# Down projections of two feed-forward blocks by seven quarter products instead of eight, with the sums of weight quarters made by adding DMAs

## The chip, the cores and the metric

The kernel runs on one core of a Trainium2 chip. Its time is device microseconds of one execution; a median of several executions is compared. TensorE (PE in the profile, PEld its weight load) does the matrix products, VectorE (DVE) and ScalarE (ACT) the element-wise work, GpSimd (POOL) some small operations, SyncE (SP) issues most DMAs. Each engine runs its own instructions in a fixed order and waits for the others by semaphores.

## The reference

Two layers over 512 tokens of width 1024, all in float32. Layer 0 mixes tokens by retention and neighbourhood attention, layer 1 by a state-space scan (SSD); the changed code is in the feed-forward block that follows each mixer.

```python
def conv_geglu_ffn(hn, w_up, conv_w, conv_b, w_down):
    u = depthwise_conv_centered(hn @ w_up, conv_w, conv_b)
    gate, val = jnp.split(u, 2, axis=-1)
    return (jax.nn.gelu(gate, approximate=True) * val) @ w_down

def reference(x, ...):
    for layer in range(DEPTH):              # 2
        hn = rms_norm(x, norm_mix_pre[layer])
        m = retention_na_mixer(hn, ...) if layer % 2 == 0 else ssd_mixer(hn, ...)
        x = x + rms_norm(m, norm_mix_post[layer])
        f = conv_geglu_ffn(rms_norm(x, norm_ffn_pre[layer]), ffn_w_up[layer], ffn_conv_w[layer],
                           ffn_conv_b[layer], ffn_w_down[layer])
        x = x + rms_norm(f, norm_ffn_post[layer])
    return x
```

The down projection is H (512 tokens x 2816) times w_down (2816 x 1024).

## The kernel before

The program is written in the order mixer 0, `ffn` of layer 0, mixer 1, `ffn` of layer 1; a tile scheduler derives each engine's order from it and from priorities, and sets the semaphores. Tokens lie in four tiles of 128 (t = 0 to 3), the inner dimension in k-tiles of 128.

Every large matrix product is made of three: each operand is split into a high part (rounded to the matmul's reduced float32, by a ScalarE copy) and a low part (what is left, by a VectorE subtract; `split`, L95 and L96), and `mm3` (L104 to L106) sums high x high, low x high and high x low in one PSUM bank.

Weights come as tiles of 128 x 1024 float32 (512 KiB) through `wload`: SP issues the load into one of three staging buffers (`wst`), `wunit` splits it into one of four pairs `whi`/`wlo`, with `high_priority(60)`, so that these splits stand early in the orders of ScalarE and VectorE.

In `ffn` the up projection goes over 22 steps f; a step computes gate and value columns (128 each) for all 512 tokens, 2 x 8 x 3 = 48 matmuls of 512 columns. `tail` does the convolution, the GELU and the product, and splits the result at once into `hh` and `hl`, the k-tile f of H.

`down_tm` then computes the down projection by halves n of 512 output columns: for each batch of weight tiles, four token tiles, 22 k-tiles x 3 matmuls in a bank per token tile and half. That is 528 matmuls of 128 x 512 for each layer. The last batch has six weight tiles, whose last parts are put in buffers of H that are free (`extra`). After a half of a token tile, `post_half` takes the sum of squares (ScalarE, Square, `junk`) and the product with the gain (VectorE, `mg`). `finish` has the steps x (`post_norm`: residual), s (the pre-norm of what follows, or the store of the output) and t (`turn`: eight TensorE transposes into `pt`, split into the residents `xh`/`xl`, from which the next mixer or projection reads). A norm goes through POOL twice: `r_m` and `r_x` are the inverse roots. Their places:

```python
DOWN = ("x0 s0", "x1 s1 t0", "x2 s2 t1", "x3 s3")
LATE = ("t2", "t3")
```

t0 is turned after token tile 1's part of the last batch, t2 and t3 are left to the following stage (`E.late`, `flush`).

Where they stand beside the change: in mixer 0 `project` makes a projection and its rotary part, in which POOL multiplies a rotated copy `rb` (L444) after SP's DMAs `rb<-ra`; in mixer 1 `project` makes the projections of a group, and POOL adds squares (`sq`). POOL issues no DMA.

## Time and profile before

| what | value |
|---|---|
| time of three executions | 1411.16 us median, 1410.93 to 1412.15 |
| span of the profiled execution | 1409.7 us |
| granted TensorE clock | 0.999 |
| PE, PEld, DVE, ACT, POOL busy | 1386.0, 1144.1, 905.1, 710.4, 62.7 us |
| DMA | 166.36 MB, mean 118 GB/s |
| matmuls of the down projections | 2 x 528 |

The span runs from the first to the last instruction of one profiled execution; the time around it is in the timed runs too. Busy matmul time is modelled and overlaps, so it is a sign of TensorE being fed and no peak rate. In a group's row the columns are line, engine, operation, names out<-in, shapes and count, then busy us and mean ns of one, then the idle time of the engine before them and who ended it. In a timeline row the first two numbers are start and length in us, and the bracket is the idle time before it with what ended it.

### The profile page before, as it was taken

How to read it: one execution, taken by the hardware profiler on the slowest of the kernel's cores; microseconds unless marked ns; L12 is line 12 of the kernel's file. 1: busy time of each engine (PE TensorE's matmuls, PEld its weight loads, DVE VectorE, ACT ScalarE, POOL GpSimd, SP SyncE). 2: the span in 40 equal slices, each digit the busy share in tenths (PEclk: the TensorE clock that was granted, in tenths of full speed). 3: DMA queues.
4: the chain of work that ended last, by engine and by line, in shares of the span. 5: the costliest groups of instructions: out<-in, count | busy, mean ns of one | idle time of the engine just before them, and what ended most of it. 6: DMA issues, size and time to landing. Idle time of an engine off the chain costs nothing.

```text
span 1409.7 us, 18020 instructions
## 1 busy us (share of the span) xinstructions
PE 1386.0 (98%) x6908; PEld 1144.1 (81%) x6908; DVE 905.1 (64%) x1364; ACT 710.4 (50%) x1203; POOL 62.7 (4%) x66
## 2 busy tenths in 40 slices
PE   7999999999999999999999999999999999999998
PEld 6877787898888888888778787787888888888886
DVE  7378888755566652347878786897786565654232
ACT  5356665544444431324877787477454444442230
POOL 0010110100000000000000110010110000000000
PEclk9999999999999999999999999999999999999999
DMA  8443233222333233333566454273433333232231
GB/s 291 147 141 96 87 97 101 86 86 92 103 91 104 90 90 109 115 113 106 142 185 189 136 182 146 75 212 107 137 120 105 105 90 105 91 105 90 90 105 60
DMA packets 56438, 166.36 MB, mean 118 GB/s; under 512 B 6688, under 2 KB 7456, under 8 KB 56352
## 3 DMA queue, kind: packets, MB, share of 16 engines
q1 hardware_dynamic: 48464, 150.00, 34.0%
q10 hardware_dynamic: 7888, 15.21, 3.8%
q8 instruction: 55, 0.90, 0.3%
q14 instruction: 31, 0.25, 0.1%
HBM read 157.57 MB, written 5.51 MB: 116 GB/s over the span
## 4 chain that ended last, share of the span: by engine, by line
PE 88%; DVE 4%; ACT 3%; DMA 2%; issue 1%; POOL 1%; SPq 0%; DVEq 0%; POOLq 0%; ACTq 0%
PE mm L104 26%; PE mm L106 26%; PE mm L105 26%; PE pi L844 1%; PE st L793 1%; PE py L864 1%; PE pt L161 1%; PE pt L737 1%; PE y L519 1%; ACT pb L823 1%; DMA pb<-pd 0%; ACT junk L141 0%; DMA x<-in_x 0%; DVE wlo L96 0%; ACT whi L95 0%
## 5 line engine op out<-in xcount | busy, mean ns | idle before, releaser
L104 PE MATMUL mm<-xh,whi 128*128 128x512 f32 (+1 forms) x1216 | 463.9, 382 | 0.4 <-ACT xh L95 0.2
L105 PE MATMUL mm<-xh,wlo 128*128 128x512 f32 (+2 forms) x1216 | 462.8, 381 | 1.4 <-DVE wlo L96 1.4
L106 PE MATMUL mm<-xl,whi 128*128 128x512 f32 (+2 forms) x1216 | 463.2, 381 | 0.5 <-DVE xl L96 0.5
L96 DVE TENSOR_TENSOR wlo<-wst,whi 128x1024 fp32r<-128x1024 f32 (+1 forms) x208 | 254.3, 1224 | 137.3 <-ACT whi L95 135.6
L95 ACT CAST whi<-wst 128x1024 fp32r<-128x1024 f32 (+1 forms) x208 | 216.6, 1042 | 147.1 <-PE mm L105 117.7
L104 PEld LDWEIGHTS mm<-xh,whi 128*128 128x128 f32 x1216 | 228.3, 188 | 45.2 <-issue 2.5
L105 PEld LDWEIGHTS mm<-xh,wlo 128*128 128x128 f32 (+1 forms) x1216 | 228.4, 188 | 44.7 <-DVE wlo L96 1.9
L106 PEld LDWEIGHTS mm<-xl,whi 128*128 128x128 f32 (+1 forms) x1216 | 228.1, 188 | 45.0 <-issue 1.3
L251 DVE SCALAR_TENSOR_TENSOR cv<-mm,cwt,cv 128x511 f32<-128x511 f32 x88 | 65.9, 749 | 146.2 <-ACT cv L250 146.2
L250 ACT ACTIVATE cv<-mm,cwt 128x512 f32<-128x512 f32 x88 | 68.7, 780 | 124.5 <-PE mm L106 124.5
L104 PE MATMUL mm<-whi,hh 128*128 128x512 f32 x288 | 112.0, 389 | 0.0
L105 PE MATMUL mm<-whi,hl 128*128 128x512 f32 x288 | 112.0, 389 | 0.0
L106 PE MATMUL mm<-wlo,hh 128*128 128x512 f32 x288 | 112.0, 389 | 0.0
L823 ACT ACTIVATE pb<-pb,tok 128x128 f32<-128x128 f32 x256 | 80.7, 392 | 6.9 <-DMA pb<-pd 5.5
L95 ACT CAST hh<-cv 128x512 fp32r<-128x512 f32 x44 | 27.3, 621 | 103.7 <-DVE cv L259 103.7
L252 DVE SCALAR_TENSOR_TENSOR cv<-mm,cwt,cv 128x511 f32<-128x511 f32 x88 | 66.0, 750 | 3.0
L105 PEld LDWEIGHTS mm<-whi,hl 128*128 128x128 f32 x288 | 54.1, 188 | 11.3
L104 PEld LDWEIGHTS mm<-whi,hh 128*128 128x128 f32 x288 | 54.1, 188 | 11.2
L106 PEld LDWEIGHTS mm<-wlo,hh 128*128 128x128 f32 x288 | 54.1, 188 | 11.2
L757 DVE SCALAR_TENSOR_TENSOR xf<-mm,cwt,xf 128x511 f32<-128x511 f32 (+1 forms) x64 | 47.5, 744 | 6.4 <-ACT xf L754 5.9
L96 DVE TENSOR_TENSOR hl<-cv,hh 128x512 fp32r<-128x512 f32 x44 | 30.5, 693 | 28.9 <-ACT hh L95 28.9
L141 ACT ACTIVATE junk<-mm 128x512 bf16<-128x512 f32 x24 | 14.3, 596 | 67.4 <-PE mm L106 67.3
(267 smaller groups left out, 1871.7 us busy)
## 6 DMA issues: line engine op xcount, KB each, us to landing
wst<-in_f_up SPq DMA_DIRECT2D x88, 512.0 KB
wst<-in_f_down SPq DMA_DIRECT2D x44, 512.0 KB
wst<-in_c_fm SPq DMA_DIRECT2D x40, 512.0 KB
pb<-pd ACTq DMA_DIRECT2D x29, 512.0 KB
wst<-in_ab_fm SPq DMA_DIRECT2D x20, 512.0 KB
gain<-yd SPq DMA_DIRECT2D x32, 256.0 KB
wst<-in_c_out SPq DMA_DIRECT2D x16, 512.0 KB
gain<-in_norms SPq DMA_DIRECT2D x8, 512.0 KB
```

Of the source, the lines that this page charges most:

```text
L95: first = self.nc.scalar.copy(hi, src)
L96: second = self.nc.vector.tensor_tensor(lo, src, hi.bitcast(F32), op=ALU.subtract)
L104: mm(out, lh, rh, start=first, stop=False)
L105: mm(out, ll, rh, start=False, stop=False)
L106: mm(out, lh, rl, start=False, stop=last)
L141: self.nc.scalar.activation(self.junk[:, :w], src, AF.Square, scale=float(n) ** -0.5, accum_out=s)
L161: last = nc.tensor.transpose(pt[:, j], xs[:, j * P:(j + 1) * P], self.ident)
L250: nc.scalar.activation(o, ps, AF.Identity, scale=w(1), bias=w(3))
L251: nc.vector.scalar_tensor_tensor(o[:, 1:], ps[:, :S - 1], w(0), o[:, 1:], op0=ALU.mult, op1=ALU.add)
L252: nc.vector.scalar_tensor_tensor(o[:, :S - 1], ps[:, 1:], w(2), o[:, :S - 1], op0=ALU.mult, op1=ALU.add)
L757: nc.vector.scalar_tensor_tensor(r[:, a], ps[:, b], wc(j), r[:, a], op0=ALU.mult, op1=ALU.add)
L823: nc.scalar.activation(pb[:, dr, c], pb[:, dr, c], AF.Identity, scale=1.0 - 2 * dr, bias=tok[:, 0, c, dr * H + h:dr * H + h + 1])
```

## The change

H stays float32 as `H`, unsplit. `down_strassen` cuts H into four quarters (lower and upper 256 tokens, first and second 11 k-tiles) and w_down into four quarters (11 k-tiles x 512 columns). Seven products of quarters (or of sums of quarters) replace the eight; each has 11 k-tiles x 2 token tiles x 3 = 66 matmuls, 462 for each layer. Products are numbered 0 to 6 in the order of `seq`.

- Weight sides: products 0, 3 and 6 read quarters of w_down, products 1, 2, 4 and 5 read sums from a DRAM tile `ts`. `sums` lists 32 DMAs ("chores") per layer of 704 KiB each: 16 plain copies from w_down into `ts`, and 16 that add to `ts` in DRAM. POOL issues them, and `E.chore` makes each wait for the last matmul of the projection emitted before (`E.product`). 15 of layer 0's stand in mixer 0 and 17 in the up projection of layer 0, followed there by 12 of layer 1's; the other 20 of layer 1's stand in mixer 1.
- H sides: `prepare` makes the operand of the next product after the second weight tile of a product: `raw` combines quarters on VectorE (products 1, 2 and 6; operations of 2816 columns), and two splits (1280 and 1536 columns) make it high and low. Odd products use `xh`/`xl`'s memory, even ones a pair b1h/b1l. The first operand is split during the up projection, at f = 14.
- Each product loads five weight tiles of 1024 columns and one of 512; every fourth staging tile is an extra one, `wx`.
- Results: the six banks of products 0 to 2 are copied to `k00` to `k21` (ScalarE), and later products' banks are added to them (VectorE, L380); product 6's banks hold the rest. `post_half` takes a sign.
- Turns: t0's transposes stand after the first token tile of product 6 (before its second token tile's first weight tile), t1's before its fourth weight tile. Six weight tiles of product 6 are all asked for ahead of it, two of them into free memory (`x1`, `x2`).
- At the end of mixer 1, t3's transposes stand 8 to 11 matmuls of 256 columns earlier in the next up projection.

```diff
+    def operands(self):
+        self.xh, self.xl = (self.res.tile([P, KD, S], R32, name=n, tag=n) for n in ("xh", "xl"))
+    def chore(self, n=1):
+        for _ in range(min(n, len(self.chores))):
+            self.together([self.chores.pop(0)()], [self.product])
...
-    def mm3(self, out, lh, ll, rh, rl, first, last):
-        mm = self.nc.tensor.matmul
+    def mm3(self, out, lh, ll, rh, rl, first, last, more=False):
+        mm = partial(self.nc.tensor.matmul, skip_group_check=True) if more else self.nc.tensor.matmul
         mm(out, lh, rh, start=first, stop=False)
         mm(out, ll, rh, start=False, stop=False)
-        mm(out, lh, rl, start=False, stop=last)
+        self.product = mm(out, lh, rl, start=False, stop=last)
...
-        (eng or nc.vector).tensor_tensor(m, ps, g_post[:, n * 512:(n + 1) * 512], op=ALU.mult)
-        halves.append((s, m, r))
+        halves = st.setdefault(t, {})
+        for other, _ in halves.values():
+            halves["r"] = self.inv_rms("m", other, s), None
+            break
+        gs = g_post[:, n * 512:(n + 1) * 512]
+        if sign == 1.0:
+            (eng or nc.vector).tensor_tensor(m, ps, gs, op=ALU.mult)
+        else:
+            nc.vector.scalar_tensor_tensor(m, ps, sign, gs, op0=ALU.mult, op1=ALU.mult)
+        halves[n] = s, m
...
+def quarters(w, i):
+
+    return [w[i, 2 * P * S * u:2 * P * S * (u + 1)].rearrange("(p c) -> p c", p=P) for u in range(HK // 2)] + \
+        [w[i, 2 * P * S * (HK // 2):QUARTER].rearrange("(p c) -> p c", p=P)]
+
+def sums(E, w, ts):
+
+    gp = E.nc.gpsimd
+    rows, n = QUARTER // 1024, 4
+    part = lambda a, i, c: a[i].rearrange("(r e) -> r e", e=1024)[c * rows // n:(c + 1) * rows // n]
+    out = []
+    for stage in (((0, w, 0, None), (1, w, 1, None), (2, w, 3, None), (3, w, 2, None)),
+                  ((0, w, 1, ALU.add), (1, w, 3, ALU.add)), ((2, ts, 0, ALU.add),), ((3, ts, 2, ALU.add),)):
+        for i, src, j, op in stage:
+            for c in range(n):
+                kw = dict(accum_op=op, max_dma_last_dim=4096) if op else {}
+                out.append(lambda i=i, src=src, j=j, c=c, kw=kw: gp.dma_start(part(ts, i, c), part(src, j, c), **kw))
+    return out
+
+def down_strassen(E, pool, w, ts, H, first, g_post, done):
+
+    nc, tc = E.nc, E.tc
+    lower, upper = slice(0, HW), slice(HW, S)
+    A11, A21 = H[:, :HK, upper], H[:, :HK, lower]
+    A12, A22 = H[:, HK:, upper], H[:, HK:, lower]
+    k0 = [0]
+
+    def stage(i, u, cols):
+        st = pool.tile([P, 1024], F32, name="wx") if k0[0] % 4 == 3 else E.wst.tile([P, 1024], F32, name="wst")
+        k0[0] += 1
+        nc.sync.dma_start(st[:, :cols], quarters(*i)[u])
+        return st[:, :cols]
+
+    def weights(i, u, extra=None):
+        cols = 1024 if u < HK // 2 else 512
+        st = stage(i, u, cols)
+        if extra is None:
+            hi, lo = E.whi.tile([P, 1024], R32, name="whi"), E.wlo.tile([P, 1024], R32, name="wlo")
+        else:
+            hi, lo = extra[:, :1024], extra[:, 1024:]
+        with tc.high_priority(60):
+            E.split(hi[:, :cols], lo[:, :cols], st)
+        return [(hi[:, c:c + 512], lo[:, c:c + 512]) for c in range(0, cols, 512)]
+
+    a, bb = ([E.mm.tile([P, 512], F32, name="mm") for _ in range(2)] for _ in range(2))
+    s3 = pool.tile([P, HK, HW], F32, name="s3")
+    d = []
+
+    def raw(i):
+        tt, stt = nc.vector.tensor_tensor, nc.vector.scalar_tensor_tensor
+        if i == 1:
+            tt(s3, A11, A21, op=ALU.subtract)
+            return s3
+        if i == 2:
+            tt(A21, A22, A21, op=ALU.subtract)
+            stt(A11, A11, -1.0, A21, op0=ALU.mult, op1=ALU.subtract)
+            return A11
+        if i == 6:
+            stt(A11, A12, -1.0, A11, op0=ALU.mult, op1=ALU.subtract)
+            return A11
+        return {3: A12, 4: A21, 5: A22}[i]
+
+    def prepare(i):
+        if i % 2:
+            hi, lo = (E.res.tile([P, HK, HW], R32, name="a" + n, tag=n) for n in ("xh", "xl"))
+        else:
+            hi, lo = (pool.tile([P, HK, HW], R32, name="a" + n, tag=n) for n in ("b1h", "b1l"))
+        src = raw(i)
+        for c in (slice(0, 5), slice(5, HK)):
+            E.split(hi[:, c], lo[:, c], src[:, c])
+        return hi, lo
+
+    seq = ((w, 0), a), ((ts, 1), bb), ((ts, 2), a), ((w, 2), d), ((ts, 0), a), ((ts, 3), bb), ((w, 3), a)
+    kept = {}
+    st = {}
+    op, nxt = first, None
+    started = []
+    for i, (src, bank) in enumerate(seq):
+        last = i == len(seq) - 1
+        if not bank:
+            bank.extend(E.px.tile([P, 512], F32, name="pd", tag="px") for _ in range(2))
+        more = any(bank is x for x in started)
+        started.append(bank)
+
+        def mms(t, ws, u):
+            for j, w_ in enumerate(ws):
+                k = 2 * u + j
+                cc = slice(t * P, t * P + P)
+                E.mm3(bank[t], op[0][:, k, cc], op[1][:, k, cc], *w_, not more and k == 0, k == HK - 1, more)
+
+        if last:
+            ex = {4: pool.tile([P, 2048], R32, name="x1", tag="s3"), 5: pool.tile([P, 2048], R32, name="x2", tag="e2")}
+            ws = [weights(src, u, ex.get(u)) for u in range(HK // 2 + 1)]
+            for t in range(2):
+                for u, x in enumerate(ws):
+                    if (t, u) == (1, 0):
+                        E.operands()
+                        E.finish("t0", st, done)
+                    if (t, u) == (1, 3):
+                        E.finish("t1", st, done)
+                    mms(t, x, u)
+                E.post_half(st, 2 + t, 1, bank[t], g_post, sign=-1.0)
+                E.finish(f"x{2 + t} s{2 + t}", st, done)
+            continue
+        for uu in ((0,), (1,), (2,), (3,), (4, 5)):
+            ws = [(weights(src, u), u) for u in uu]
+            for t in range(2):
+                for x, u in ws:
+                    mms(t, x, u)
+            if uu == (1,):
+                nxt = prepare(i + 1)
+        op = nxt
+        for t in range(2):
+            if i in (0, 1, 2):
+                kept[i, t] = pool.tile([P, 512], F32, name=f"k{i}{t}")
+                nc.scalar.copy(kept[i, t], bank[t])
+            else:
+                j, tok, n = {3: (0, 2, 0), 4: (1, 0, 1), 5: (2, 0, 0)}[i]
+                m = kept[j, t]
+                nc.vector.tensor_tensor(m, bank[t], m, op=ALU.add)
+                E.post_half(st, tok + t, n, m, g_post, m=m, sign=1.0 - 2 * n)
+                if i == 5:
+                    E.finish(f"x{t} s{t}", st, done)
+    E.late += [lambda s=s: E.finish(s, st, done) for s in LATE]
...
-            nc.vector.tensor_tensor(v, g, v, op=ALU.mult)
-            h = (hp.tile([P, S], R32, name="hh"), hp.tile([P, S], R32, name="hl"))
-            E.split(*h, v)
-            hs.append(h)
-
-        extra = lambda i=0: [hp.tile([P, S], R32, name=n) for n in ("hh", "hh", "hl", "hl")]
+            nc.vector.tensor_tensor(H[:, f], g, v, op=ALU.mult)
...
             tail(f, *ps)
+            E.chore(2 if f < HK else 1)
+            if f == HK + 3:
+                first = [cp.tile([P, HK, HW], R32, name="a" + n, tag=n) for n in ("b1h", "b1l")]
+                for k in range(0, HK, 4):
+                    c = slice(k, min(k + 4, HK))
+                    E.split(first[0][:, c], first[1][:, c], H[:, c, HW:])
         g_post = E.bcast(g_post_row)
-        batches = [[(0, u)] for u in (2, 2, 2, 2, 2, 1)] + [[(1, u)] for u in (2, 2, 1, 6)]
-        down_tm(E, batches, w_down, lambda k: hs[k], g_post, done, lambda i: extra() if i not in (2, 3) else None)
+        down_strassen(E, cp, w_down, ts, H, first, g_post, done)
...
         def project(p, o, nm):
             i = ("rk", "rq", "rg", "nq", "nk").index(nm)
+            E.chore(p > 0)
...
         def project(o, i, ps=None):
...
+            E.chore(i > 1)
...
+        ts = [E.dram.tile([4, QUARTER], F32, name=f"ts{i}") for i in range(2)]
+        E.chores = sums(E, ffns[0][2], ts[0])
         mixer0(E, w0, *ab, norms[0, 1], then(norms[0, 2]))
-        ffn(E, *ffns[0], norms[0, 3], then(norms[1, 0]))
+        E.chores += sums(E, ffns[1][2], ts[1])
+        ffn(E, *ffns[0], ts[0], norms[0, 3], then(norms[1, 0]))
...
+        E.chore(len(E.chores))
-        ffn(E, *ffns[1], norms[1, 3], store, w1)
+        ffn(E, *ffns[1], ts[1], norms[1, 3], store, w1)
```

How it moves instructions. First TensorE at the end of layer 0's down projection. Before, t0's transposes (`pt<-head,xs`) stand in the last batch, 36 matmuls behind token tile 0's last one:

```order
L104 MATMUL mm<-hh 128x512
L105 MATMUL mm<-hh,hl 128x512
L106 MATMUL mm<-hl,hh 128x512
L161 MATMUL pt<-head,xs 128x128 x8
L104 MATMUL mm<-hh 128x512
```

After, they stand in product 6 (left operand in `ab1h`, `ab1l`), 35 matmuls behind the end of product 5:

```order
L116 MATMUL mm<-whi,ab1h 128x512
L117 MATMUL mm<-whi,ab1l 128x512
L173 MATMUL pt<-head,xs 128x128 x4
L118 MATMUL mm<-wlo,ab1h 128x512
L173 MATMUL pt<-head,xs 128x128 x4
L116 MATMUL mm<-whi,ab1h 128x512
```

Both sets of four stand one matmul apart, and a matmul of product 6 is between them.

Second, VectorE at the same place (L96 is L108 after the change, the subtract of a split; L127 is L139, L199 is L218, L152 is L164). Before, the splits of the last batch stand first, and then t0's chain:

```order
L96 TENSOR_TENSOR hl_4932<-wst_4933,hh_4930 128x512
L96 TENSOR_TENSOR wlo_5221<-wst_5218,whi_5220 128x1024
L96 TENSOR_TENSOR wlo_5227<-wst_5224,whi_5226 128x1024
L127 TENSOR_SCALAR v_m_4978<-ssm0_4699,ssm1_4975 128x1
L175 TENSOR_TENSOR mg_4977<-mm_4745,gain_4381 128x512
L199 SCALAR_TENSOR_TENSOR x_97<-mg_4701,r_m_4980,x_97 128x512
L199 SCALAR_TENSOR_TENSOR x_97<-mg_4977,r_m_4980,x_97 128x512
L152 SCALAR_TENSOR_TENSOR xs_4991<-x_97,r_x_4989,gain_4985 128x512
L152 SCALAR_TENSOR_TENSOR xs_4993<-x_97,r_x_4989,gain_4985 128x512
```

After, the add of product 5's bank to `k20` (L380) is followed by four splits of product 6's weights, and only then by the chain:

```order
L380 TENSOR_TENSOR k20_4682<-mm_4344,k20_4682 128x512
L108 TENSOR_TENSOR x1_5067<-wst_5093,x1_5067 128x1024
L108 TENSOR_TENSOR wlo_5084<-wst_5081,whi_5083 128x1024
L108 TENSOR_TENSOR wlo_5090<-wx_5087,whi_5089 128x1024
L108 TENSOR_TENSOR x2_5068<-wst_5097,x2_5068 128x512
L139 TENSOR_SCALAR v_m_5032<-ssm1_4913,ssm0_5030 128x1
L191 TENSOR_TENSOR k20_4682<-k20_4682,gain_4340 128x512
L218 SCALAR_TENSOR_TENSOR x_97<-k10_4570,r_m_5034,x_97 128x512
L218 SCALAR_TENSOR_TENSOR x_97<-k20_4682,r_m_5034,x_97 128x512
L380 TENSOR_TENSOR k21_4684<-mm_4345,k21_4684 128x512
L164 SCALAR_TENSOR_TENSOR xs_5045<-x_97,r_x_5043,gain_5039 128x512
L164 SCALAR_TENSOR_TENSOR xs_5047<-x_97,r_x_5043,gain_5039 128x512
```

Both orders keep the chain's own steps; four splits and the second token tile's add have come into it.

Third, POOL in mixer 0. Before:

```order
L444 TENSOR_TENSOR rb<-rb,rot 128x512 x3
L533 TENSOR_TENSOR rs<-rs,rg 128x512
L444 TENSOR_TENSOR rb<-rb,rot 128x512 x2
L533 TENSOR_TENSOR rs<-rs,rg 128x512
L444 TENSOR_TENSOR rb<-rb,rot 128x512 x2
```

After, chores stand between them:

```order
L601 TENSOR_TENSOR rb<-rb,rot 128x512 x2
L274 DMA ts_222<-in_f_down 16x11264 x2
L601 TENSOR_TENSOR rb<-rb,rot 128x512
L274 DMA ts_222<-in_f_down 16x11264
L690 TENSOR_TENSOR rs<-rs,rg 128x512
L274 DMA ts_222<-in_f_down 16x11264
L601 TENSOR_TENSOR rb<-rb,rot 128x512
L274 DMA ts_222<-in_f_down 16x11264 x3
L601 TENSOR_TENSOR rb<-rb,rot 128x512
```

POOL's own operations keep their order; each chore between them waits for a projection's last matmul.

36 lines of the change are left out of this document (23 added, 13 removed).

## The prediction

> **What bounds the kernel now.** I read the page's first lines, then the busy time by stages, then the timeline at the places that the change touches.
>
> ```profile
> PE 1386.0 (98%) x6908; PEld 1144.1 (81%) x6908; DVE 905.1 (64%) x1364; ACT 710.4 (50%) x1203; POOL 62.7 (4%) x66
> ...
> PEclk9999999999999999999999999999999999999999
> ...
> PE 88%; DVE 4%; ACT 3%; DMA 2%; issue 1%; POOL 1%; SPq 0%; DVEq 0%; POOLq 0%; ACTq 0%
> PE mm L104 26%; PE mm L106 26%; PE mm L105 26%; PE pi L844 1%; PE st L793 1%; PE py L864 1%; PE pt L161 1%; PE pt L737 1%; PE y L519 1%; ACT pb L823 1%; DMA pb<-pd 0%; ACT junk L141 0%; DMA x<-in_x 0%; DVE wlo L96 0%; ACT whi L95 0%
> ```
>
> TensorE is busy 98% of the span at full granted clock, and 88% of the chain that ends last is its work, 78% in the three lines of a product. A removed matmul should therefore shorten the run by its own spacing, if nothing else becomes late. The stages (stretch in us; length; busy us of PE, PEld, DVE, ACT, POOL with counts; clock; DMA share; GB/s):
>
> ```profile
> 290.00:492.00 202.00, 202.00 (x926) 168.69 (x926) 124.32 (x153) 90.35 (x116) 0.00 (x0) 1.00 0.30 94
> 492.00:612.00 120.00, 120.00 (x531) 99.38 (x530) 44.86 (x50) 36.09 (x50) 0.00 (x0) 1.00 0.36 112
> 612.00:660.00 48.00, 47.76 (x296) 42.08 (x295) 28.58 (x47) 19.14 (x33) 4.39 (x8) 1.00 0.22 81
> 740.00:850.00 110.00, 110.00 (x573) 89.61 (x572) 85.98 (x124) 87.47 (x187) 8.71 (x5) 1.00 0.55 169
> 1285.00:1405.00 120.00, 118.50 (x523) 97.78 (x521) 36.14 (x45) 25.53 (x40) 1.94 (x4) 1.00 0.26 84
> ```
>
> The first two are layer 0's up and down projections, the third its end into layer 1's mixer, the last is layer 1's down projection. In both down stages TensorE never waits, while VectorE is busy 45 of 120 us. The change shortens exactly these stages and fills VectorE there.
>
> **What a removed matmul is worth.** 22 k-tiles x 4 token tiles x 2 halves x 3 = 528 matmuls per layer become 7 products x 11 x 2 x 3 = 462: 66 fewer per layer, 132 in all. Their row gives 389 ns each:
>
> ```profile
> L104 PE MATMUL mm<-whi,hh 128*128 128x512 f32 x288 | 112.0, 389 | 0.0
> ```
>
> But matmuls overlap. What counts is start to start, and the last token tiles give it: each ScalarE Square waits for a token tile's 36 matmuls.
>
> ```profile
> 1387.28 0.60 ACT L141 ACTIVATE junk<-mm 128x512 bf16<-128x512 f32 x1 [7.47 <-PE mm L106]
> ...
> 1395.44 0.60 ACT L141 ACTIVATE junk<-mm 128x512 bf16<-128x512 f32 x1 [7.47 <-PE mm L106]
> ...
> 1403.60 0.60 ACT L141 ACTIVATE junk<-mm 128x512 bf16<-128x512 f32 x1 [7.47 <-PE mm L106]
> ```
>
> The Squares stand 8.16 us apart, 8.16 / 36 = 226.7 ns. So 132 x 0.2267 = **-29.9 us**; taken by the 389 ns it would be -51, which double counts the overlap. The Trainium skill ("TensorE: Matmul & The Clock Gate", section Back-to-back issue gap) gives about 131 ns for a matmul of 512 columns in a sustained stream, and calls the longer formula, about 216 ns, an isolated gap. By 131 ns the saving would be estimated at 17.3 us and the sum at 1402 us, which speaks against this change. This trace shows the longer spacing in a sustained stream; the measurement decides, and the sum keeps the row.
>
> **Inside the down projections: does VectorE keep up?** Durations (line, engine, operation, shape, count | busy, mean ns | idle before):
>
> ```profile
> L96 DVE TENSOR_TENSOR wlo<-wst,whi 128x1024 fp32r<-128x1024 f32 x207 | 253.7, 1226 | 137.3 <-ACT whi L95 135.6
> L95 ACT CAST whi<-wst 128x1024 fp32r<-128x1024 f32 x207 | 216.0, 1044 | 146.8 <-PE mm L105 117.4 <-PE mm L106 10.0 <-DMA wst<-in_f_down 6.9
> L96 DVE TENSOR_TENSOR hl<-cv,hh 128x512 fp32r<-128x512 f32 x44 | 30.5, 693 | 28.9 <-ACT hh L95 28.9
> L259 DVE TENSOR_TENSOR cv<-cv,cv 128x512 f32<-128x512 f32 x44 | 30.2, 685 | 0.6 <-DVE cv L252 0.5
> L95 ACT CAST hh<-cv 128x512 fp32r<-128x512 f32 x44 | 27.3, 621 | 103.7 <-DVE cv L259 103.7
> L199 DVE SCALAR_TENSOR_TENSOR x<-mg,r_m,x 128x512 f32<-128x512 f32 x32 | 22.8, 749 | 2.3 <-POOL r_m L134 0.9 <-DMA x<-xd 0.4
> ```
>
> Two sizes (512: 0.685, 1024: 1.226 us) give 0.144 + 1.057 ns per column. A 2816-column operand combination is then about 3.1 us, the two splits of an operand (1280 and 1536 columns) 1.50 + 1.77 = 3.3 us. One product lasts 66 x 0.2267 = 14.96 us on TensorE. VectorE needs in it 5 x 1.226 + 0.69 = 6.8 us for weights, 3.3 for the next operand, 0 to 6.4 for combinations (none, one or two; they are for products 1, 2 and 6) and up to 2.9 for adding a kept bank and scaling it (2 x 0.685 + 2 x 0.749). That is 10 to 16.5 us by product, about 94 of 105 us in all, against 45 of 120 before. So it fits on average but not in each product; product 1 and product 5 have the least room. There the four hi/lo weight pairs in flight are the cushion: by the VectorE order, the third weight of product 1 comes 0.6 us before it is needed, and the following ones 0.8 to 4. I put **+0.6 us** on both layers for short waits; bounds 0 and, if each of the 12 product starts slips by 2 us (one late combination less the cushion), 24. The first because TensorE had no idle in 492 to 612; I stay near it, since its margins are positive row by row. ScalarE needs about 10.5 of 15 us per product (weights 5.8, operand splits 2.7, two bank copies 1.2, Squares) and is covered. The splits of H (44 x (0.693 + 0.621) us) leave the up stage, where TensorE was 100% busy: worth nothing. The first operand's splits move into it: VectorE is busy 124 of 202 there, worth nothing.
>
> **Layer 0's end into layer 1's mixer.** This is where I expect a new wait. In the stage before, the chain of one token tile from its Square to its normed rows:
>
> ```profile
> 611.37 0.60 ACT L141 ACTIVATE junk<-mm 128x512 bf16<-128x512 f32 x1 [6.71 <-PE mm L106]
> 612.09 0.21 DVE L127 TENSOR_SCALAR v_m<-ssm,ssm 128x1 f32<-128x1 f32 x1 [6.18 <-ACT junk L141]
> 612.38 0.55 POOL L134 TENSOR_TENSOR r_m<-v_m,head 128x1 f32<-128x1 f32 x1 [332.12 <-DVE v_m L127]
> 612.97 1.42 DVE L199 SCALAR_TENSOR_TENSOR x<-mg,r_m,x 128x512 f32<-128x512 f32 x2
> 614.48 1.06 ACT L141 ACTIVATE junk<-x 128x1025 bf16<-128x1025 f32 x1 [2.42 <-DVE x L199]
> 615.70 0.55 POOL L134 TENSOR_TENSOR r_x<-ssx,head 128x1 f32<-128x1 f32 x1 [2.77 <-ACT junk L141]
> 616.29 1.41 DVE L152 SCALAR_TENSOR_TENSOR xs<-x,r_x,gain 128x512 f32<-128x512 f32 x2 [1.91 <-POOL r_x L134]
> ```
>
> ```profile
> 619.34 1.03 PE L161 MATMUL pt<-head,xs 128*128 128x128 f32 x8
> ...
> 628.65 0.60 ACT L141 ACTIVATE junk<-mm 128x512 bf16<-128x512 f32 x1 [4.80 <-PE mm L106]
> ...
> 643.22 1.03 PE L161 MATMUL pt<-head,xs 128*128 128x128 f32 x8
> ```
>
> That is 6.3 us (611.37 to 617.70) with VectorE free. t0's transposes came 8.0 us after its Square (at 619.34), t2's 14.6 us (628.65 to 643.22): nothing waited. After, t0's stand 35 matmuls (7.9 us) into product 6, and ahead of its chain stands work with priority: ScalarE's casts, and VectorE's subtracts, of product 6's third to sixth weight. Two of them wait for a pair that product 5 frees only at its end, then follow 2 x 1.04 + 0.6 us of casts, and only then the Square. Counted from product 5's end the chain ends at about 9.8 us (3.5 + 6.3), TensorE is there at 7.9: **+1.9**. t1's has a few tenths of room. t2's transposes stand 36 matmuls and 16 transposes behind its bank (about 10.7 us instead of 14.6), and its Square, both norms and its xs stand behind t1's rows and two or three weight splits of the mixer (1.23 us each) on both engines: ready at some 22 us, against 19.5 on TensorE, and t1's low part, which the next matmul reads, half a us later: **+3.0**. Bounds for the two together: 0 (only 0.24 us of idle in 612 to 660 before) and 10 (each of the four turns late by 2.5). I take 4.9, by these rows in their new order.
>
> **Mixer 1 into layer 1's up projection.** t3's transposes now stand 8 to 11 short matmuls (0.12 us each) earlier, and TensorE already waited for them:
>
> ```profile
> 1052.07 0.63 PE L161 MATMUL pt<-head,xs 128*128 128x128 f32 x4 [0.69 <-DVE xs L152]
> ```
>
> About 1 us more of the same wait, partly given back later: **+0.7**, bounds -0.5 (the later stream gets shorter) and +2.
>
> **The 64 adding and copying DMAs.** Each moves 704 KiB within DRAM, issued by POOL after a projection's last matmul. In layer 0's mixer they stand between the rotary adds (L444) and the gate products on POOL; in mixer 1 between the sq adds; the norms' r_m and r_x come after the last chore of their stage. No such DMA is in this trace. Nearest rows:
>
> ```profile
> 10.00:14.00 4.00, 3.00 (x16) 2.25 (x15) 4.00 (x6) 3.93 (x8) 0.55 (x1) 1.00 1.03 420
> ...
> q1 hardware_dynamic: 48464, 150.00, 34.0%
> ...
> 587.71 2.13 SPq L64 DMA_DIRECT2D wst<-in_f_down  x3
> ...
> 591.46 1.05 ACT L95 CAST whi<-wst 128x1024 fp32r<-128x1024 f32 x1 [3.47 <-DMA wst<-in_f_down]
> ...
> L444 POOL TENSOR_TENSOR rb<-rb,rot 128x512 f32<-128x512 f32 x8 | 12.1, 1518 | 136.1 <-DMA rb<-ra 136.1
> ```
>
> At the peak of 420 GB/s a chunk takes 1.7 us; at the mean of the busy queue, 150 MB in 34% of 1409.7 us = 313 GB/s, three streams (two reads, a write) take 6.9 us. All 64 then occupy the DMA engines some 110 to 440 us of 1400, where the share is 0.3 to 0.55. A weight is loaded three ahead and used 3.75 us after issue, a product consumes one in 2.7 us, so a doubled latency is still covered. POOL waits for DMAs anyway (136 us before the L444 rows); a chore ahead of one costs its issue and its wait for the product, which comes within the same projection. I take **+2**; bounds 0 (hidden) and 8 (about 0.3 us at each of 24 projections with a chore in front of a POOL step).
>
> **The sum.** -29.9 + 0.6 + 4.9 + 0.7 + 2.0 = -21.7. Kept banks, signs (749 instead of 685 ns) and the end after the last matmul (1403.60 to 1409.7 as before) change under 0.2. The profiled span is 1409.7, the median of the runs 1411.16, 1.5 more, which lies around the span: 1411.2 - 21.7 = **1389.5 us**. A measurement of this kernel can tell about 0.2% (2.8 us) from no change.
>
> **Rivals.** *Cover is better than I count* (chance 0.14): the transposes at the boundary wait little and the DMAs are free: -29.9 + 1 to 2 leaves **1383 us**. For it: the scheduler's order leaves the same work to be done after the wait. Against: the priority splits stand ahead of the norm rows.
> *A removed matmul is worth less than its spacing* (0.02): if the stream is paced by something that the products keep, only what is left goes; the lowest that a row here bears is one weight load, 10.9 us for 48 matmuls being 227 ns while the load is busy 99.38 us / 530 = 188 ns: 132 x 0.188 = 24.8 gives **1395 us**. Against: load and matmul go together, and the spacing is even. (The Trainium skill's 131 ns, above, would be this case taken further.)
> *VectorE becomes the bound of the down stages* (0.17): products 1, 2, 5, 6 start late because the combination of 3 to 6 us stands in front of weight splits; 12 starts x 1 to 2 us = 12 to 24, giving **1401 to 1411 us**. For it: up to 16.5 us of work in 14.96. Against: about 94 of 105 in sum and four pairs in flight.
> *The adding DMAs are late* (0.07, the other side): product 5 of layer 0 reads the last sum. Its 16 adds are issued two per up-projection step (10.9 us each: 8 x 6 matmuls); from the first of them 8 x 10.9 of issue, 120 of the up stage's rest and 5 x 15 of products pass, 282 us, 17.6 us for each add if they go one by one. Above 19.1 us (38 GB/s) 16 x 1.5 = 24 eats the gain and it is slower; at 22 us it is 16 x 4.4 = 70, **1460 us**. Against: the busy queue above runs at 313 GB/s. The Trainium skill ("DMA: Bandwidth & Descriptors", section Anatomy of one DMA) gives 2.0 us plus bytes / 436 GB/s for a DMA that POOL issues; by that an estimate for a chunk would be 3.7 us. No run here shows it yet.
>
> **Chances.** The forecast (1384 to 1396) 0.60, better cover 0.14, cheaper matmuls 0.02, VectorE 0.17, late adds 0.07. Faster by over 0.2%: 0.60 + 0.14 + 0.02 + 0.15 = 0.91; same 0.02; slower 0.07. The range holds the forecast, better cover and the nearer half of the VectorE case: **1382 to 1402 us**.
>
> **What would show it.** Right: 6776 PE instructions and about 105 us per down stage; Square to Square 7.48 us in product 6 (33 matmuls); a wait of 1 to 3 us on xs before the transposes at layer 0's end; VectorE over 85% in the down stages; chunks of under 7 us. Wrong: idle of PE on wlo, or on the low part of an operand, at the start of products 1, 5 or 6 by over 1 us each; PE waiting for in-mixer loads or for rb; weights of product 1 that come behind the adds.

## The result, and the profile after

The changed kernel takes 1427.05 us (1425.02 to 1429.76) against 1411.66 us for the one before (1410.93 to 1414.88): a ratio of 1.0104, interval 1.0086 to 1.0121. It is 1% slower, where 1389.5 us was forecast and 1402 us was the upper end. The page of its profiled execution (span 1424.7 us):

```profile
PE 1370.3 (96%) x6776; PEld 1128.4 (79%) x6776; DVE 987.8 (69%) x1402; ACT 758.3 (53%) x1233; POOL 109.8 (8%) x130
...
PEclk9999999999999999999989998999999999999999
...
PE 79%; DMA 6%; DVE 6%; ACT 4%; issue 3%; POOL 1%; SPq 0%; DVEq 0%; POOLq 0%; ACTq 0%
PE mm L116 23%; PE mm L117 23%; PE mm L118 23%; DMA pb<-pd 4%; PE st L951 1%; PE pi L1002 1%; DVE wlo L108 1%; PE pd L117 1%; PE pd L116 1%; PE pd L118 1%; PE pt L173 1%; PE py L1022 1%; ACT whi L107 1%; ACT pb L981 1%; PE pt L894 1%
...
ts<-in_f_down POOLq DMA_DIRECT2D x48, 704.0 KB, 5.6
...
ts<-ts POOLq DMA_DIRECT2D x16, 704.0 KB, 10.3
```

The 132 matmuls are gone (6908 to 6776), but TensorE sits idle for 1424.7 - 1370.3 = 54 us instead of 24, and its busy time fell by only 15.7. In the chain the load `pb<-pd` has grown from 0% to 4% (some 57 us); it belongs to mixer 1, and the change does not touch it. The last two rows are the new DMAs: 5.6 us median from issue to landing for those that read w_down (32 copies and 16 adds), 10.3 us for the 16 adds from `ts` to `ts`.

Where this lies is read from rows that give the first and the last start of a group. Before: the tails of the up projections (L259), mixer 1's first `z`, the last pre-norm (`xs`, the end of mixer 1).

```profile
L259 DVE TENSOR_TENSOR cv<-cv,cv x44: 683/684/693, 297.5 to 1287.7; 128x512 f32<-128x512 f32 x44
...
L677 ACT ACTIVATE z<-mm,bc x2: 467/469/471, 662.7 to 663.2; 64x256 f32<-64x256 f32 x2
...
L152 DVE SCALAR_TENSOR_TENSOR xs<-x,r_x,gain x32: 743/748/754, 6.6 to 1051.8; 128x512 f32<-128x512 f32 x32
```

After:

```profile
L408 DVE TENSOR_TENSOR H<-cv,cv x44: 683/684/692, 301.3 to 1319.5; 128x512 f32<-128x512 f32 x44
...
L834 ACT ACTIVATE z<-mm,bc x2: 470/471/472, 658.0 to 658.5; 64x256 f32<-64x256 f32 x2
...
L164 DVE SCALAR_TENSOR_TENSOR xs<-x,r_x,gain x32: 742/747/754, 6.5 to 1077.5; 128x512 f32<-128x512 f32 x32
```

From these rows, and from the same rows of the experiments' profiled executions below (us; e3's profiled execution is the longest of its four, and 307.3 is part of that, so its mixer 1 is what to read):

| kernel | mixer 0 (to the first tail) | layer 0's up and down (to the first z) | mixer 1 (to the last xs) | layer 1's up (to the last tail) | layer 1's down (to the end) | span |
|---|---|---|---|---|---|---|
| before | 297.5 | 365.2 | 389.1 | 235.9 | 122.0 | 1409.7 |
| after | 301.3 | 356.7 | 419.5 | 242.0 | 105.2 | 1424.7 |
| e1, no chores in mixer 1 | 300.5 | 357.1 | 390.7 | 240.5 | 105.8 | 1394.6 |
| e2, chores in up stages only | 298.1 | 357.2 | 391.0 | 240.2 | 105.8 | 1392.3 |
| e3, small chores | 307.3 | 356.9 | 391.0 | 241.8 | 105.2 | 1402.2 |
| e4, before with the chores | 297.4 | 365.1 | 417.1 | 235.8 | 122.4 | 1437.8 |
| e5, copies instead of adds | 302.2 | 355.6 | 398.7 | 242.1 | 105.2 | 1403.8 |
| e6, adds spaced | 300.6 | 355.6 | 411.2 | 242.2 | 105.8 | 1415.4 |
| e8, own pool | 298.2 | 356.5 | 391.8 | 238.7 | 105.0 | 1390.2 |

The two stretches that end in a down projection gain 8.5 and 16.8 us. Mixer 1, whose matmuls are the same, loses 30.4. TensorE's waits there (engine, line, for whom: us in total, times, longest):

```profile
PE mm L116 <- DVE xf L915: 8.7, 2, 8.5
PE mm L116 <- ACT z L921: 8.1, 1, 8.1
PE pt L894 <- ACT bf L924: 4.6, 1, 4.6
```

The names are VectorE's and ScalarE's, but both engines stand behind ScalarE's use of `pb`: the wait of 8.1 us ends at 722.09, after ScalarE's wait for `pb` at 719.69 below, and the one of 8.5 us after two such waits, which end at 862.25 and 869.82. ScalarE's own waits for that load, before and then after:

```profile
ACT pb L823 <- DMA pb<-pd: 5.5, 3, 2.3
```

```profile
ACT pb L981 <- DMA pb<-pd: 34.3, 9, 7.6
```

One of them, on ScalarE's timeline. ScalarE issues two loads of 512 KiB (ACTq row) and uses the first. Before it is 5.9 us (706.79 to 712.66):

```profile
706.79 0.95 ACTq L812 DMA_DIRECT2D pb<-pd  x2
712.66 0.40 ACT L823 ACTIVATE pb<-pb,tok 128x128 f32<-128x128 f32 x1 [2.02 <-DMA pb<-pd]
```

After it is 10.7 us (708.96 to 719.69), with one chore issued at 706.31 in flight:

```profile
708.96 1.01 ACTq L970 DMA_DIRECT2D pb<-pd  x2
719.69 0.40 ACT L981 ACTIVATE pb<-pb,tok 128x128 f32<-128x128 f32 x1 [7.64 <-DMA pb<-pd]
```

Around this place the stretches of 2 us show TensorE's stop and what it costs beyond itself (after PE, PEld, DVE, ACT and POOL come granted clock, DMA share and GB/s):

```profile
712.00:714.00 2.00, 1.97 (x21) 1.61 (x16) 1.88 (x4) 0.05 (x1) 0.00 (x0) 1.00 0.98 246
714.00:716.00 2.00, 0.00 (x0) 0.00 (x0) 1.02 (x2) 0.00 (x0) 0.00 (x0) 1.00 0.65 91
716.00:718.00 2.00, 0.00 (x0) 0.00 (x0) 0.00 (x0) 0.00 (x0) 0.00 (x0) 0.74 1.03 332
718.00:720.00 2.00, 0.00 (x0) 0.00 (x0) 0.00 (x0) 0.31 (x1) 0.00 (x0) 0.50 1.07 263
...
724.00:726.00 2.00, 2.00 (x6) 1.63 (x5) 1.04 (x2) 2.00 (x8) 0.00 (x0) 0.50 0.03 8
726.00:728.00 2.00, 2.00 (x7) 1.56 (x7) 0.76 (x1) 1.98 (x7) 0.00 (x0) 0.70 0.00 0
728.00:730.00 2.00, 2.00 (x10) 1.64 (x9) 0.49 (x1) 1.46 (x2) 0.00 (x0) 1.00 0.04 8
```

TensorE stops for 8 us. About 3 us into the stop the granted clock falls to 0.50, and for some 5 us after the stop the matmuls run at half speed: 12 of them take 5.2 us (722.09 to 727.31) instead of 2.7, which costs 2.5 us. The mean clock of the execution is 0.985, against 0.999 before. The Trainium skill ("TensorE: Matmul & The Clock Gate", Part 1) says that the clock halves after an idle window of about 3.4 us and comes back after a busy one as long. This trace agrees in kind: the fall comes about 3 us into the stop, and the half clock behind it lasts some 5 us, longer than one such window.

The DMA share was at its limit here before the change already, for a few us at a time:

```profile
695.00:700.00 5.00, 5.00 (x24) 3.10 (x23) 4.72 (x7) 5.00 (x14) 0.00 (x0) 1.00 0.97 242
700.00:705.00 5.00, 5.00 (x22) 3.08 (x21) 5.00 (x10) 4.98 (x18) 0.00 (x0) 1.00 1.03 234
...
710.00:715.00 5.00, 5.00 (x40) 4.04 (x38) 1.91 (x3) 2.90 (x5) 0.00 (x0) 1.00 0.99 240
```

The stage's mean of 0.55 hid that.

### The profile page after: what moved, and what is told of

It is laid out like the page before. It is cut to its first block, busy times and chain, and to the rows that moved or that the text cites. A ratio compares the mean times of both kernels' runs of the same rounds, so it can differ in the third digit from the quotient of the medians.

```text
span 1424.7 us, 18086 instructions
## 1 busy us (share of the span) xinstructions
PE 1370.3 (96%) x6776; PEld 1128.4 (79%) x6776; DVE 987.8 (69%) x1402; ACT 758.3 (53%) x1233; POOL 109.8 (8%) x130
## 4 chain that ended last, share of the span: by engine, by line
PE 79%; DMA 6%; DVE 6%; ACT 4%; issue 3%; POOL 1%; SPq 0%; DVEq 0%; POOLq 0%; ACTq 0%
PE mm L116 23%; PE mm L117 23%; PE mm L118 23%; DMA pb<-pd 4%; PE st L951 1%; PE pi L1002 1%; DVE wlo L108 1%; PE pd L117 1%; PE pd L116 1%; PE pd L118 1%; PE pt L173 1%; PE py L1022 1%; ACT whi L107 1%; ACT pb L981 1%; PE pt L894 1%
## 5 line engine op out<-in xcount | busy, mean ns | idle before, releaser
L116 PE MATMUL mm<-xh,whi 128*128 128x512 f32 (+1 forms) x1216 | 467.4, 385 | 16.8 <-DVE xf L915 8.5
L108 DVE TENSOR_TENSOR wlo<-wst,whi 128x1024 fp32r<-128x1024 f32 (+1 forms) x232 | 280.4, 1212 | 68.7 <-ACT whi L107 68.0
L107 ACT CAST whi<-wst 128x1024 fp32r<-128x1024 f32 (+1 forms) x232 | 238.5, 1031 | 96.2 <-PE mm L117 68.1
L981 ACT ACTIVATE pb<-pb,tok 128x128 f32<-128x128 f32 x256 | 81.2, 393 | 35.7 <-DMA pb<-pd 34.3
L117 PE MATMUL mm<-whi,ab1l 128*128 128x512 f32 x164 | 64.5, 394 | 0.0
L116 PE MATMUL mm<-whi,ab1h 128*128 128x512 f32 x164 | 64.4, 393 | 0.0
L118 PE MATMUL mm<-wlo,ab1h 128*128 128x512 f32 x164 | 63.8, 389 | 0.0
L274 POOL DMA_DIRECT2D ts<-in_f_down x48 | 30.8, 644 | 355.5 <-PE mm L118 351.0
L406 ACT ACTIVATE cv<-cv 128x512 f32<-128x512 f32 x44 | 27.8, 633 | 42.1 <-DVE cv L401 42.1
L117 PE MATMUL mm<-whi,yl 128*128 128x512 f32 x104 | 41.1, 395 | 0.0
L116 PE MATMUL mm<-whi,yh 128*128 128x512 f32 x104 | 40.8, 394 | 0.2 <-DVE xf L915 0.2
L118 PE MATMUL mm<-wlo,yh 128*128 128x512 f32 x104 | 40.6, 390 | 0.0
## 6 DMA issues: line engine op xcount, KB each, us to landing
ts<-ts POOLq DMA_DIRECT2D x16, 704.0 KB, 10.3
```

Of the source, the lines that this page charges most:

```text
L107: first = self.nc.scalar.copy(hi, src)
L108: second = self.nc.vector.tensor_tensor(lo, src, hi.bitcast(F32), op=ALU.subtract)
L116: mm(out, lh, rh, start=first, stop=False)
L117: mm(out, ll, rh, start=False, stop=False)
L118: self.product = mm(out, lh, rl, start=False, stop=last)
L274: out.append(lambda i=i, src=src, j=j, c=c, kw=kw: gp.dma_start(part(ts, i, c), part(src, j, c), **kw))
```

## The experiments

Theory after the result: the chores' bytes take the DMA engines from the `pb<-pd` loads of mixer 1, which ScalarE issues only some 6 us ahead of their use. Rivals: the chores' waits on POOL in front of its `sq` and `rg` (rival POOL), or something in the Strassen code itself, its buffers or its order (rival products).

**e1: layer 1's chores in its own up projection.**

```diff
-        E.chores += sums(E, ffns[1][2], ts[1])
-        E.chore(len(E.chores))
+        E.chores = sums(E, ffns[1][2], ts[1])       # ahead of layer 1's ffn
-            E.chore(2 if f < HK else 1)
+            E.chore(2)
```

> All 32 chores of layer 1 are issued in layer 1's own up projection, two per step, none in mixer 1; layer 0's stay. Theory (the chores' bytes take the DMA engines from the pb<-pd loads in mixer 1): mixer 1 is about 30 us shorter, 1392 to 1401 us. Rival POOL (the chores' waits in front of POOL's sq and rg make those late): the same 1397. Rival products (the loss in mixer 1 comes from the Strassen code itself, its buffers or its order): 1424 to 1429, and the pb<-pd waits stay.

1397.58 us (1396.35 to 1402.98), ratio 0.9903 (0.9875 to 0.9932). Mixer 1 takes 390.7 us, 28.8 less than after the change, and ScalarE's waits for the loads are back near the 5.5 us of before:

```profile
ACT pb L981 <- DMA pb<-pd: 6.1, 3, 2.1
```

Rival products falls.

**e2: layer 0's chores too, none in a mixer.** As e1, with `E.chores = sums(E, ffns[0][2], ts[0])` behind mixer 0.

> As the one before, and layer 0's 32 chores stand in layer 0's up projection, none in mixer 0. Theory: mixer 0 gets back the 3.8 us by which it became longer, so 1389 to 1397 us, and 3 to 4 us under the one before; TensorE stays without idle in both up stages though the DMA share is near 1.0 there. Rival (mixer 0's 3.8 us are not the chores'): equal to the one before. If the last sums come late, waits on wst<-ts at products 1, 2 or 5.

1394.40 us (1391.64 to 1397.37), ratio 0.9874 (0.9848 to 0.9899). Mixer 0 is 2.4 us shorter than in e1. The difference of the medians, 3.2 us, is no more than the spread of the runs; its direction is the expected one. The profiled executions point the same way: mixer 0 takes 297.2 to 299.8 us in all that have no chores in it (e9 with 299.8 is the longest), and 300.5 to 307.3 in all that have them. TensorE has no idle in either up stage:

```profile
300.00:495.00 195.00, 195.00 (x862) 161.53 (x861) 110.76 (x130) 75.39 (x93) 22.04 (x32) 1.00 0.76 214
1070.00:1285.00 215.00, 215.00 (x950) 178.00 (x949) 122.77 (x143) 86.07 (x104) 21.96 (x32) 1.00 0.72 202
```

How much room is there shows in the changed kernel's layer 0, with two adds in each step of 10.9 us and then one copy:

```profile
320.00:400.00 80.00, 80.00 (x355) 66.26 (x354) 45.17 (x53) 31.30 (x40) 12.12 (x14) 1.00 0.97 226
420.00:520.00 100.00, 100.00 (x443) 82.83 (x442) 52.79 (x63) 37.20 (x46) 4.49 (x10) 1.00 0.49 162
```

With 0.30 before, an add takes an estimated (0.97 - 0.30) x 10.9 / 2 = 3.7 us of all DMA engines, a copy (0.49 - 0.30) x 10.9 = 2.1. TensorE is busy 80 of 80 us at a DMA share of 0.97; weights are the only loads there, and they are issued three tiles ahead.

**e3: the same waits, a sixteenth of the bytes.** The sums of layer 1 are left unfinished. Four more small adds are appended, so that mixer 1 still has 20 chores when all 16 copies stand in layer 0 (the lines below are shortened).

```diff
+    cut = lambda a: a[:a.shape[0] // 16]            # layer 1's adds only
-    gp.dma_start(part(ts, i, c), part(src, j, c), **kw)
+    gp.dma_start(cut(part(ts, i, c)), cut(part(src, j, c)), **kw)
-            E.chore(2 if f < HK else 1)
+            E.chore((2 if f < HK else 1) + (f in (12, 14, 16, 18)))   # all 16 copies in layer 0
```

> As the changed kernel, but the 20 chores of mixer 1 move a sixteenth of their bytes (sums of layer 1 are left unfinished), with the same waits for a product and the same places on POOL; layer 1's 16 copies are all in layer 0's up projection. Theory (bytes): 1393 to 1402 us, the pb<-pd waits gone. Rival POOL (waits): 1424 to 1430, nothing gained.

1397.38 us (1393.84 to 1403.97), ratio 0.9886 (0.9856 to 0.9916). Mixer 1 takes 391.0 us with all 20 POOL waits in place, and ScalarE's wait for the loads is back near the one before:

```profile
ACT pb L982 <- DMA pb<-pd: 7.3, 4, 4.6
```

Rival POOL falls: it is the bytes.

**e4: the kernel before, with the chores.** All 528 matmuls of each layer stay, and nothing reads the sums.

```diff
+            E.chore(f >= NF - 12)       # in ffn, behind tail
+            E.chore(i > 1)              # in mixer 1's project
```

> The kernel before, all its matmuls kept, with layer 1's 32 chores added: 12 copies in layer 0's last up steps, 20 chores in mixer 1 (4 copies, 16 adds) into a DRAM tile that nothing reads. Theory (bytes) and rival POOL: mixer 1 is 25 to 32 us longer, 1436 to 1445 us, with pb<-pd waits as in the changed kernel and the granted clock at half behind each long wait. Rival products: 1411 to 1414.

1442.53 us (1439.65 to 1444.22), ratio 1.0212 (1.0186 to 1.0238). Mixer 1 takes 417.1 us, 28.0 more than before, without any Strassen product in the program:

```profile
ACT pb L851 <- DMA pb<-pd: 26.4, 6, 6.8
```

So the chores alone bring nearly all of the loss (28.0 of 30.4 us), and without them it is gone (e1). That the loss passes through the `pb<-pd` loads is read from the waits. Mixer 1 is longer than before by 30.4 us after the change, 28.0 in e4, 22.1 in e6, 9.6 in e5 and 1.6 in e1, and ScalarE waits for these loads 34.3, 26.4, 30.7, 16.3 and 6.1 us: the waits go up and down with the loss, though not in proportion. They are not the only loads that are slowed: VectorE's waits for `gain<-yd` and `yd<-ysc` are 2.3 us each after the change and none before. No run issued the `pb<-pd` loads earlier.

**e5: plain copies in the adds' places** (layer 1's weight sums are not formed).

```diff
-                kw = dict(accum_op=op, max_dma_last_dim=4096) if op else {}
+                kw = dict(accum_op=op, max_dma_last_dim=4096) if op and not plain else {}
```

> As the changed kernel, but layer 1's 16 adds are plain copies of the same 704 KiB (so layer 1's weight sums are not formed): the same places, waits and bytes moved, without the second read. In the changed kernel's up stage a copy per 10.9 us raises the DMA share from 0.30 to 0.51, 2.3 us of all engines, two adds per 10.9 us raise it to about 1.0, 3.8 us each. Theory saturation (mixer 1's own share of 0.5 plus one chore per 5.44 us; an add makes 0.5 + 0.70, a copy 0.5 + 0.42): copies stay under 1 and cost 3 to 12 us of the 30, so 1400 to 1409. Rival number of chores (each chore in flight delays a pb<-pd load, whatever it does): 1422 to 1429.

1405.53 us (1403.62 to 1406.95), ratio 0.9948 (0.9929 to 0.9966). Mixer 1 takes 398.7 us: 20 copies cost 8.0 us over e1, where 4 copies and 16 adds cost 28.8. A copy costs this stage 0.4 us, an add (28.8 - 4 x 0.4) / 16 = 1.7 us, four times as much, while it takes 3.7 / 2.1 = 1.8 times the engine time; the number of chores is not what counts. The edit takes away more than the addition, though. It also drops `max_dma_last_dim`, and the queue's rows (packets, MB, share of 16 engines), of the changed kernel and then of e5, show the same bytes in fewer packets:

```profile
q0 software_dynamic: 7168, 46.14, 13.5%
```

```profile
q0 software_dynamic: 4608, 46.14, 11.5%
```

The first has 32 copies and 32 adds, the second 48 and 16, which gives 32 packets for a copy and 192 for an add. (The shares give 2.0 and 4.0 us of all engines, near the estimates above.) Whether the second read or the small packets make an add dearer was not tried apart.

**e6: the 16 adds behind every second projection.**

```diff
-            E.chore(i > 1)
+            E.chore(i > 1 and i % 2)
-            E.chore(2 if f < HK else 1)
+            E.chore((2 if f < HK else 1) + (f in (12, 14, 16, 18)))   # all 16 copies in layer 0
```

> All 16 adds of layer 1 stay in mixer 1, but behind every second projection, so 10.9 us apart and over all four groups instead of 5.4 us apart in the first two; the four copies move to layer 0's up stage. Theory saturation: 0.5 + 0.35 stays under 1, the loss in mixer 1 falls from 30 to 0 to 8 us, 1396 to 1405. Rival sum of bytes (each add costs mixer 1 the same 1.5 to 1.9 us wherever it stands): 16 x 1.7 = 27, 1420 to 1427.

1421.20 us (1417.18 to 1424.98), ratio 1.0068 (1.0044 to 1.0093). This was a miss: mixer 1 takes 411.2 us, so 20.5 of the 28.8 remain, about 1.3 us per add; by the medians it is 1421.20 - 1397.58 = 23.6, or 1.5 per add. The rival, the same price wherever an add stands, named 1420 to 1427 and holds the time; its 1.5 to 1.9 us per add is met at its lower end by the medians. That the mean share stays under 1 is no protection: it is 0.63 over mixer 1, but 0.99 from 690 to 720. On POOL's timeline one add is issued at 703.39, 25 us behind the one before it:

```profile
703.39 0.87 POOL L274 DMA_DIRECT2D ts<-in_f_down  x1 [23.92 <-PE mm L118]
```

From the issue of ScalarE's next pair of loads to the first use of them it takes 11.0 us, where it took 5.8 in e1 (701.75 to 707.54):

```profile
704.95 0.96 ACTq L970 DMA_DIRECT2D pb<-pd  x2
715.96 0.40 ACT L981 ACTIVATE pb<-pb,tok 128x128 f32<-128x128 f32 x1 [7.17 <-DMA pb<-pd]
```

SP's four loads `gain<-yd` follow 0.9 us behind the pair in both. One add, issued 1.6 us ahead of the pair, is enough. Nor were the adds evenly spaced: mixer 1's projections come in bursts, and three were issued between 739.9 and 752.1.

**e7: later turns.** As e2, t0 at (1, 2) and t1 at (1, 5) in product 6.

```diff
-                    if (t, u) == (1, 0):    # t0, with E.operands() left at (1, 0)
+                    if (t, u) == (1, 2):
-                    if (t, u) == (1, 3):    # t1
+                    if (t, u) == (1, 5):
```

> As the kernel with all chores in the up stages, and in product 6 t0's transposes stand before the second token tile's third weight tile, t1's before its sixth. Theory (t0's and t1's waits on xs, 1.2 and 0.6 us, are covered by later places): 1.5 to 3 us under it, 1391 to 1393. Rival (the chain of t2 behind them is the limit, the wait only moves to t2's transposes): equal, 1393 to 1396.

1394.57 us (1392.49 to 1396.34), ratio 0.9870 (0.9851 to 0.9890), the same as e2. Of TensorE's waits in 590 to 660, those on `xs` fall from 2.7 to 1.5 us, and the one on the mixer's weight split rises from 1.2 to 2.6:

```profile
PE mm L117 <- DVE wlo L108: 2.6, 1, 2.6
PE pt L173 <- DVE xs L164: 1.5, 2, 0.9
```

So the rival is right that the wait only moves, but it moves to `wlo` and not to t2's transposes.

**e8: the extra weight buffers in a pool of their own.** As e2.

```diff
+        xp = ctx.enter_context(tc.tile_pool(name="ffn_x", bufs=1))
         cp = ctx.enter_context(tc.tile_pool(name="ffn_c", bufs=1))
-            t = [cp.tile([P, 2048 // len(tags)], ...
+            t = [xp.tile([P, 2048 // len(tags)], ...    # b1h, b1l, e2, also in down_strassen
```

> As the kernel with all chores in the up stages, and the extra weight buffers of the up projection stand in a memory pool of their own, opened first. In the changed kernel their first split (xb1h) waits at layer 1's up projection for the release of mixer 1's memory, and TensorE waits 0.9 and 1.3 us for it. Theory: these two waits go, 1391 to 1393. Rival (behind it the transposes of t3 are the limit): equal, 1393 to 1396.

1391.30 us (1389.49 to 1391.98), ratio 0.9846 (0.9828 to 0.9863). TensorE's waits between mixer 1 and layer 1's up projection are now two:

```profile
PE pt L173 <- DVE xs L164: 1.5, 2, 0.8
PE mm L118 <- DVE xl L108: 0.5, 1, 0.5
```

The waits of 0.9 and 1.3 us for the extra weights (`xb1h`, `xb1l`) are gone, and that stage is 1.5 us shorter than in e2. This is the best version: 1.5% faster than the kernel before. Its lead over e2 is 3 us by the medians; the intervals of the ratios overlap, and e11 below repeats its time.

**e9 and e10: the norms' chains with priority.** As e8, with the add of product 5's banks and the steps of t0 to t3 under `tc.high_priority(60)`, or 120.

> As the kernel with all chores in the up stages and the extra buffers in a pool of their own (1391.3), and the add of product 5's banks, the norms of t0 to t3 in the down projection and their steps x and s get the priority of the weight splits (60): the chain of t0 no longer stands behind four splits, t2's stands ahead of a split of the mixer's weights. Theory (layer 0's end loses about 6 us of the 15 because chains stand behind splits): 2 to 4 us come back, 1387 to 1389. Rival (the wait moves to the splits, on wlo and x2): 1390 to 1394.

> The same with priority 120, so that the chains stand ahead of product 6's third and fourth weight split too. Theory: as with 60 or up to 1 us better, 1386 to 1389. Rival: TensorE waits for these splits 2.7 us into product 6, 1390 to 1395.

**e11: e8 again, beside these two.**

> The kernel with all chores in the up stages and the extra buffers in their own pool once more, beside the two above, in more rounds: 1389 to 1393; the difference to them prices the priorities.

1395.79 (1394.55 to 1396.77), 1395.93 (1394.98 to 1397.34) and 1391.80 us (1390.46 to 1392.31); the ratios are 0.9880 (0.9863 to 0.9896), 0.9884 (0.9870 to 0.9899) and 0.9853 (0.9838 to 0.9868). Both were misses: with the priorities the kernel is 4 us slower, over the theories and over the rivals. TensorE's waits for the rows of t0 and t1 fall from 1.9 us (e11) to 0.9 in e9, but a longer wait comes behind them, on a split of the mixer's weights (the operand beside it is `xh`) that now stands behind t3's steps on VectorE. The rivals had named product 6's splits; TensorE waits for these 0.4 us in e10 and not at all in e9. The mixer's wait in e9 and then in e10:

```profile
632.75 0.58 PE L117 MATMUL mm<-xh,wlo 128*128 128x256 f32 x1 [2.68 <-DVE wlo L108]
```

```profile
631.75 0.58 PE L117 MATMUL mm<-xh,wlo 128*128 128x256 f32 x1 [2.68 <-DVE wlo L108]
```

The granted clock is 0.50 from 634 to 638 in e9, and only from 630 to 632 in e11. In the profiled executions layer 0's up and down take 2.5 and 2.1 us more than in e11; another 2.6 and 1.9 us lie in mixer 0, ahead of the changed steps, and their cause is open.

## Why the prediction was wrong

**The step that failed is the term for the 64 DMAs**, +2 us with bounds 0 and 8. By e2 they cost 1427.05 - 1394.40 = 32.7 us where the change puts them, 28 to 29 us of it in mixer 1. The prices of a chunk were inside the bounds (2.1 and 3.7 us of all engines, 1.7 to 6.9 given). What failed is the next sentence, on who waits. It named the weight loads, which are issued three ahead and do ride over the chores, and POOL's own steps, which do not matter (e3). It left out the loads `pb<-pd` that ScalarE issues just before it needs them; they stand in the page of before among the DMA issues (x29, 512 KiB) and in its chain. It also used the stage's mean share of 0.55, in a stage whose share is 0.97 to 1.03 for 10 us at a time. "PE waiting for in-mixer loads" stood among the signs of being wrong, but no term of the sum priced it.

**A second step was missing**: a stop of TensorE was priced by its length. Here a stop of 8 us brought some 5 us of half clock besides, 2.5 us more. In the changed kernel PE's busy time fell by 15.7 us; in e2, where the clock is 0.997, it fell to 1359.2, by 26.8. The 11 us between them are read as the same matmuls at the lower clock: 8.7 of them are in mixer 1, where the mean clock is 0.96 against 1.00 in e2. TensorE's idle time in mixer 1 is 28.8 us against 9.0, so of the 28.5 us between the two some 20 are waiting and 9 lower clock.

**A removed matmul** was right. The Squares of the last two token tiles, 33 matmuls apart, stand 7.39 us apart, 224 ns each (226.7 used). The first of them does not wait for TensorE, so this is a little low; the two stretches shown below for VectorE give 102.00 / 450 and 78.00 / 344, both 226.7 ns.

```profile
1410.89 0.60 ACT L153 ACTIVATE junk<-mm 128x512 bf16<-128x512 f32 x1
...
1418.28 0.60 ACT L153 ACTIVATE junk<-mm 128x512 bf16<-128x512 f32 x1 [6.70 <-PE mm L118]
```

The rival of cheaper matmuls does not hold here, and neither do the 131 ns of the Trainium skill ("TensorE: Matmul & The Clock Gate", section Back-to-back issue gap).

**VectorE in the down projections** was right, and its rival (1401 to 1411 us) wrong. In the interior of the seven products TensorE is never idle, while VectorE is busy 77 and 81%, less than the 94 of 105 us that were counted and the 85% that were to be the sign:

```profile
500.00:602.00 102.00, 102.00 (x450) 84.14 (x449) 78.94 (x72) 58.81 (x68) 0.97 (x2) 1.00 0.56 180
1322.00:1400.00 78.00, 78.00 (x344) 64.31 (x344) 63.19 (x53) 47.62 (x55) 0.00 (x0) 1.00 0.61 194
```

**Layer 0's end** was forecast at +4.9. The stretch gained 8.5 us where 66 matmuls are worth 15.0: +6.5. The waits stand where they were expected, on the chains of t0, t1 and t2 and on splits of the mixer's weights:

```profile
618.82 0.66 PE L173 MATMUL pt<-head,xs 128*128 128x128 f32 x4 [1.01 <-DVE xs L164]
625.58 0.66 PE L173 MATMUL pt<-head,xs 128*128 128x128 f32 x4 [0.61 <-DVE xs L164]
...
629.64 0.39 PE L117 MATMUL mm<-xh,wlo 128*128 128x256 f32 x1 [0.41 <-DVE wlo L108]
630.78 0.38 PE L117 MATMUL mm<-xh,wlo 128*128 128x256 f32 x1 [0.75 <-DVE wlo L108]
632.06 1.94 PE L173 MATMUL pt<-head,xs 128*128 128x128 f32 x8 [0.90 <-DVE xs L164]
```

The clock right behind them:

```profile
632.00:634.00 2.00, 1.94 (x9) 1.97 (x10) 2.00 (x5) 0.59 (x1) 0.00 (x0) 0.50 0.89 342
```

The five waits are 3.7 us in sum, and the clock at 0.50 in 632 to 634 and 0.74 in 634 to 636 adds 1.5; the other 1.3 are not accounted for. t0's wait is 1.0, not 1.9. e7 and e9 show that neither later turns nor priorities bring this back; whether another order of product 6 would was not tried.

**Mixer 1 into the up projection** was forecast at +0.7; the stretch is 6.1 us longer in the changed kernel and 4.3 in e2. The transposes of t3 are a small part. 1.5 us is the wait for mixer 1's memory, which the first tile of a new, larger pool inherits (e8); the prediction did not see it. Of the 2.8 us that are left in e8 the cause stays open: part of it may be that the last tail, which ends the stretch, stands later on VectorE, since the down stage behind it gained 16.8 us where 15.0 was worked out.

**The side** (slower) was that of the rival of late adds, but by another mechanism: the sums were never late. No engine waits for a load from `ts` in the changed kernel or in e2. The DMAs that make the sums slowed other loads.

## What to carry to other kernels

Before adding DMA traffic beside a stage, list the loads that this stage issues just in time, and look at the DMA share in stretches of 2 to 5 us around them: here a mean of 0.55 hid bursts at 1.0. Put the traffic where loads are issued well ahead; here the same 64 DMAs cost 33 us less when all of them ran beside the up projections, where TensorE never waited. A long stop of TensorE is to be priced with the half-speed stretch behind it.
